# A batched matmul whose output stores are cut into even and odd partitions and spread around the x load

## Chip, cores, metric

One Trainium2 chip, one core. The metric is the device time of one execution in microseconds. A ratio is the mean time of one kernel's fast runs over the mean of the other's of the same rounds, so it is not quite the ratio of the medians that are quoted.

## The reference

```python
b1, b2, m, k, n = 8, 16, 256, 512, 384
# x: (b1, b2, m, k) float32, weight: (b1, b2, k, n) float32
np.matmul(x, weight).astype(np.float32)
```

These are 128 independent products of 256x512 by 512x384. 168 MB are read and 50 MB written.

## The kernel before

Four products (G = 4) make a group, and there are 32 groups. A group has two weight loads of 1.5 MB, one x load of 2 MB and one store of 1.5 MB. All are issued in program order by SyncE on one queue, and the loads run four groups ahead (LAG = 4). VectorE casts the weights, ScalarE casts x, TensorE transposes x through PSUM and multiplies, and ScalarE copies the result to `out_sb`. The matmuls work on 32 columns of the array each, four of them side by side, one for each product of the group; the page has 4096 of them, of 342 ns on average, in 185.1 us of busy TensorE, so they overlap in the records.

```python
def load(e, t, U, s):
    n = t * U + s
    for d in range(G // D):                       # two weight loads
        ...
            e.wait_ge(w_cast, n * (G * S) + ((d + 1) * D * S - 2 * G * S))
        e.dma_start(w_sb[slot][:], ...).then_inc(w_in[slot], 16)
    ...
        e.wait_ge(x_cast, n * T + (1 - XS) * T)   # x of two groups earlier is cast
    e.dma_start(x_sb[s % XS][:], ...).then_inc(x_in[s % XS], 16)

def store(e, t, U, s, pieces=1):
    n = t * U + s
    dram = o_rows[...].rearrange("(p r) n -> p r n", r=R)
    for q in range(pieces):
        rows = slice(q * R // pieces, (q + 1) * R // pieces)
        e.wait_ge(o_copied, n * T + ((q + 1) * T // pieces + BIAS))
        e.dma_start(out=dram[:, rows], in_=out_sb[s % OS][:, rows]).then_inc(o_out[s % OS], 16)

def multiply(e, t, U, s):
    ...                                           # 16 transposes, then:
    for q in range(T):                            # T = 4
        ...
        for rr in range(2):
            for ko in range(KO):                  # KO = 4
                for i in range(G):
                    mine = slice(i * C, (i + 1) * C)          # 32 columns
                    ins = e.matmul(po[...][mine, rr, :N], x_t[...][..., mine, ko % 2],
                                   w_bf[(s * G + i) % WBS][:, ko, :],
                                   start=(ko == 0), stop=(ko == KO - 1))

def on_sync(e):
    for n in range(LAG):
        load(e, 0, NG, n)
    with e.Fori(0, rounds) as t:
        for s in range(U):
            load(e, t, U, LAG + s)
            store(e, t, U, s)
    for n in range(rounds * U, NG):               # the last stores
        ...
```

## Time and profile before

| | before |
|---|---|
| time, median of the runs | 518.4 to 518.7 us, by batch |
| bytes, packets on the queue | 218.11 MB, 18864 |
| share of the queue, mean rate | 99.3%, 422 GB/s |
| busiest compute engine | VectorE, 64% |

A packet is what one DMA engine moves in one go, here one partition's row: 12 KB for weights and outputs (12160 packets in the records), 16 KB for x (4096). Two things of the trace stand outside the page. The packet records have a start and a length for each packet, but not its engine. The landing records have 16 counts for each transfer (2096 for 131 transfers); I take each for one engine's, made as its share lands. I call the time from the first of the 16 to the last the lag of the last engine.

### The profile page before, as it was taken

What the parts mean: (1) busy time and instruction counts of PE and PEld (TensorE: products, weight loads), DVE (VectorE), ACT (ScalarE), POOL (GpSimd) and SP (SyncE); (2) the same over time, 40 slices, a digit from 0 to 9 for tenths busy, and PEclk for the clock granted to TensorE, in tenths of its full rate; (3) what the DMA queues carried; (4) which work ended last, traced back from release to release, by engine and by line L of the source; (5) the groups of instructions that cost most, each with busy time, mean ns of one, the idle gap of its engine ahead of it and who ended that gap; (6) DMA issues with size and microseconds to landing.
All of it is one profiled execution on the core that took longest, in us unless ns stands there. A gap on an engine that the chain in (4) does not pass through costs nothing.

```text
span 517.2 us, 11523 instructions
## 1 busy us (share of the span) xinstructions
PE 306.6 (59%) x4608; PEld 200.6 (39%) x4608; DVE 332.8 (64%) x384; ACT 236.7 (46%) x264; POOL 0.7 (0%) x6
## 2 busy tenths in 40 slices
PE   0478776556665457645577554776446765467752
PEld 0345444334443334433344332444324443244431
DVE  3698875667556676556675566855658656676550
ACT  0465564443644436435355354454444544544441
POOL 0000000000000000000000000000000000000000
PEclk9998877878777887878777778877788877778777
DMA  8999999999999999999999999999999999999996
GB/s 340 430 423 424 424 432 426 429 428 430 432 427 427 427 428 432 429 427 430 426 431 431 426 429 430 427 432 427 427 429 429 427 433 425 430 428 430 429 428 251
DMA packets 18869, 218.18 MB, mean 422 GB/s; under 512 B 2096, under 2 KB 2096, under 8 KB 2608
## 3 DMA queue, kind: packets, MB, share of 16 engines
q1 hardware_dynamic: 18864, 218.11, 99.3%
q8 instruction: 3, 0.05, 0.0%
q14 instruction: 2, 0.02, 0.0%
HBM read 167.77 MB, written 50.33 MB: 422 GB/s over the span
## 4 chain that ended last, share of the span: by engine, by line
DMA 81%; ACT 10%; PE 4%; issue 3%; ACTq 0%; SPq 0%
DMA x_sb<-in_x_dram 81%; ACT x_bf L132 9%; PE po L180 2%; PE pt L166 1%; ACTq L130 0%; ACT out_sb L194 0%; SPq L111 0%; SPq L103 0%; ACT L132 0%; ACTq L193 0%; SPq L282 0%; SPq L55 0%
## 5 line engine op out<-in xcount | busy, mean ns | idle before, releaser
L147 DVE CAST w_bf<-w_sb 64x1536 bf16<-64x1536 f32 x256 | 244.4, 955 | 47.2 <-DMA w_sb<-in_weight_dram 38.5
L166 PE MATMUL pt<-identity,x_bf 128*128 128x128 f32 x512 | 123.7, 425 | 199.3 <-ACT x_bf L132 199.1
L180 PE MATMUL po<-w_bf,x_t 128*32 128x384 bf16 x4096 | 185.1, 342 | 1.0 <-issue 1.0
L166 PEld LDWEIGHTS pt<-identity,x_bf 128*128 128x128 f32 x512 | 91.8, 216 | 232.1 <-issue 218.3
L194 ACT COPY out_sb<-po 128x768 f32<-128x768 f32 x128 | 102.2, 798 | 147.2 <-PE po L180 147.2
L153 DVE COPY x_t<-pt 128x1024 bf16<-128x1024 bf16 x128 | 88.4, 691 | 122.3 <-PE pt L166 121.8
L132 ACT CAST x_bf<-x_sb 128x1024 bf16<-128x1024 f32 x128 | 124.4, 1042 | 80.9 <-DMA x_sb<-in_x_dram 80.8
L180 PEld LDWEIGHTS po<-w_bf,x_t 128*32 128x32 bf16 x4096 | 108.8, 101 | 73.8 <-issue 14.2
L132 ACT ACT_TABLE_LOAD x8 | 10.3, 1283 | 42.9 <-DMA x_sb<-in_x_dram 42.9
masks.py:199 POOL TENSOR_SCALAR_AFFINE_SELECT identity<-identity 128x128 f32<-128x128 f32 x1 | 0.3, 292 | 0.2 <-POOL identity L200 0.2
L200 POOL MEMSET identity<- 128x128 f32 x1 | 0.2, 204 | 0.5 <-SPq L55 0.5
L271 POOL MEMSET const-bfloat16-1.0<- 128x1 bf16 x1 | 0.1, 101 | 0.0
L271 POOL MEMSET const-uint8-127<- 128x1 uint8 x1 | 0.1, 101 | 0.0
L271 POOL MEMSET const-float32-0.0<- 128x1 f32 x1 | 0.1, 98 | 0.2 <-issue 0.2
L271 POOL MEMSET const-float32-1.0<- 128x1 f32 x1 | 0.1, 98 | 0.0
## 6 DMA issues: line engine op xcount, KB each, us to landing
w_sb<-in_weight_dram SPq DMA_DIRECT2D x64, 1536.0 KB, 27.5
x_sb<-in_x_dram SPq DMA_DIRECT2D x32, 2048.0 KB, 27.5
out_dram<-out_sb SPq DMA_DIRECT2D x31, 1536.0 KB, 30.7
out_dram<-out_sb SPq DMA_DIRECT2D x4, 384.0 KB, 5.9
```

What stands on the lines that cost most here:

```text
L132: e.copy(out=x_bf[s % BS][:, rows], in_=x_sb[s % XS][:, rows].rearrange("p r (q s c) -> p r s q c", s=S, c=KO),).then_inc(x_cast, 1)
L147: e.tensor_copy(out=w_bf[(s * G + d * D + a) % WBS][h * HP : (h + 1) * HP], in_=w_sb[slot][a * HP : (a + 1) * HP, h * KO : (h + 1) * KO, : ...
L153: e.tensor_copy(out=x_t[s % TS][:, 2 * q : 2 * q + 2], in_=pt[(s * T + q) % PT][:].bitcast(bf16),).then_inc(t_copied, 1)
L166: ins = e.transpose(pt[(s * T + q) % PT][:, rr, h, :], words[:, 2 * q + rr, h :: KO // 2], identity[:],)
L180: ins = e.matmul(po[(s * T + q) % PO][mine, rr, :N], x_t[s % TS][:, 2 * q + rr, ko // 2, mine, ko % 2], w_bf[(s * G + i) % WBS][:, ko, :], ...
L194: e.copy(out=out_sb[s % OS][:, 2 * q : 2 * q + 2, :], in_=po[(s * T + q) % PO][:, :, :N],).then_inc(o_copied, 1)
L200: e.memset(identity[:], 0.0).then_inc(id_done, 1)
L271: nc = _bacc.Bacc("TRN2", target_bir_lowering=False, num_devices=1)
```

## The change

The writes are spread: half of each store, the even partitions, goes between the weights and x of a later group, the other half, the odd ones, behind x. Below they are the even half and the odd half.

```diff
-    def load(e, t, U, s):
+    def load_w(e, t, U, s):
...
+    def load_x(e, t, U, s):
...
-    def store(e, t, U, s, pieces=1):
+    def store(e, t, U, s, half=None, pieces=1):
...
+        parts = slice(0, P) if half is None else slice(half, P, 2)
...
+            e.dma_start(
+                out=dram[parts, rows], in_=out_sb[s % OS][parts, rows]
+            ).then_inc(o_out[s % OS], 16)
...
             for s in range(U):
-                load(e, t, U, LAG + s)
-                store(e, t, U, s)
+                load_w(e, t, U, LAG + s)
+                store(e, t, U, s, half=0)
+                load_x(e, t, U, LAG + s)
+                store(e, t, U, s, half=1)
```

The counts of `o_out` go from 16 to 32 a store. The stores of the tail are halved too, but the last one still goes in four pieces by rows.

More of the change, by code (lines that the diff above doesn't have):

```diff
@@ L108, in load @@
             ).then_inc(w_in[slot], 16)
+    def load_x(e, t, U, s):
+        n = t * U + s
         if not isinstance(n, int) or n >= XS:
@@ L121, in store @@
             e.wait_ge(o_copied, n * T + ((q + 1) * T // pieces + BIAS))
-            e.dma_start(out=dram[:, rows], in_=out_sb[s % OS][:, rows]).then_inc(
-                o_out[s % OS], 16
-            )
+            e.dma_start(
+                out=dram[parts, rows], in_=out_sb[s % OS][parts, rows]
+            ).then_inc(o_out[s % OS], 16)
     def cast_x(e, t, U, s, q):
@@ L191, in copy_out @@
         if q == 0:
-            e.wait_ge(o_out[s % OS], (t * (U // OS) + s // OS) * 16 + 16)
+            e.wait_ge(o_out[s % OS], (t * (U // OS) + s // OS) * 32 + 32)
         e.wait_ge(p_made, n * T + (q + 1 + BIAS))
@@ L207, in on_sync @@
         for n in range(LAG):
-            load(e, 0, NG, n)
+            load_w(e, 0, NG, n)
+            load_x(e, 0, NG, n)
         rounds = (NG - LAG) // U
@@ L211, in on_sync @@
             for s in range(U):
-                load(e, t, U, LAG + s)
-                store(e, t, U, s)
-        for n in range(rounds * U, NG):
-            if n + LAG < NG:
-                load(e, 0, NG, n + LAG)
-            store(e, 0, NG, n, T if n == NG - 1 else 1)
+                load_w(e, t, U, LAG + s)
+                store(e, t, U, s, half=0)
+                load_x(e, t, U, LAG + s)
+                store(e, t, U, s, half=1)
+        for n in range(rounds * U, NG - 1):
+            for half in range(2):
+                store(e, 0, NG, n, half=half)
+        store(e, 0, NG, NG - 1, pieces=T)
         for s in range(OS):
-            e.wait_ge(o_out[s], 16 + 16 * (NG // OS + (T - 1 if s == (NG - 1) % OS else 0)))
+            e.wait_ge(o_out[s], 32 + 32 * (NG // OS) + (16 * (T - 2) if s == (NG - 1) % OS else 0))
     def on_vector(e):
@@ L242, in on_scalar @@
         for s in range(OS):
-            e.sem_inc(o_out[s], 16)
+            e.sem_inc(o_out[s], 32)
         with e.Fori(0, NG // U) as t:
```

## The prediction

> **What bounds the kernel now.** I read the share of the DMA queue first, then the slices, then the chain of waits, then the issues.
>
> ```profile
> span 517.2 us, 11523 instructions
> ...
> DMA  8999999999999999999999999999999999999996
> GB/s 340 430 423 424 424 432 426 429 428 430 432 427 427 427 428 432 429 427 430 426 431 431 426 429 430 427 432 427 427 429 429 427 433 425 430 428 430 429 428 251
> ...
> q1 hardware_dynamic: 18864, 218.11, 99.3%
> ...
> DMA 81%; ACT 10%; PE 4%; issue 3%; ACTq 0%; SPq 0%
> ```
>
> One queue moves 218.11 MB, and the time of its packets is 99.3% of all 16 DMA engines' span. Every slice but the first and the last holds 423 to 433 GB/s. No compute engine comes near: the busiest, VectorE, has 64%. So this is a DMA-bound kernel, with about 1% outside the packets. The chain "DMA 81%, ACT 10%" must not be read as a latency to be cut: it is a chain of x loads that mostly stand in a queue that is already full, as these two views show.
>
> ```profile
> w_sb<-in_weight_dram SPq DMA_DIRECT2D x64, 1536.0 KB, 27.5
> x_sb<-in_x_dram SPq DMA_DIRECT2D x32, 2048.0 KB, 27.5
> out_dram<-out_sb SPq DMA_DIRECT2D x31, 1536.0 KB, 30.7
> ```
>
> and two rounds of the chain in order of time (start, length):
>
> ```profile
> 433.75 2.94 ACT x_bf L132 x3
> ...
> 436.86 27.73 DMA x_sb<-in_x_dram
> ...
> 465.65 2.94 ACT x_bf L132 x3
> ...
> 468.88 27.67 DMA x_sb<-in_x_dram
> ```
>
> An x load takes 27.7 us from issue to landing, but 2 MB over 16 engines is 8 packets of 16 KB on each, and one such packet takes 0.611 us in the packet records: 4.9 us of work, 22.8 us of queue. The step of that chain, 468.88 - 436.86 = 32.0 us, is the time of two groups (there are two x buffers). Two groups of DMA work are 2 x (16 + 8) packets of 12 KB at 0.460 us and 2 x 8 of 16 KB at 0.611: 22.1 + 9.8 = 31.9 us. The chain runs at the pace of the queue, to 0.1 us.
>
> **The floor.** From the packet records: each engine carries 760 packets of 12 KB (64 weight loads and 31 stores, 8 each), mean 462.3 ns, smallest 459; 256 of 16 KB, mean 614.4, smallest 608; 32 of 3 KB at 121; 131 semaphore packets at 9. Sum: 351.4 + 157.3 + 3.9 + 1.2 = 513.7 us. With every packet at its usual least (460 and 611) it would be 349.6 + 156.4 + 5.1 = 511.1. The first packet starts 2.0 us into the span and the slowest engine's last one ends at about 515.4; 1.8 us of completion follow. In two engines whose packets I could follow one by one, a store packet takes 460.0 ns (461 for the first of eight on one of them) between load packets of 460 to 466: changing direction costs nothing that could be saved. So no reordering of the same bytes can gain more than some 5 us, 1%; 2% would need 508.2.
>
> [...]
>
> **The change part by part.** Removed: 31 stores of 1.5 MB. Added: 62 of 0.75 MB, each four packets of 12 KB on each engine; bytes and packet sizes stay. Each group has one more semaphore packet: 31 x 9 ns = 0.28 us per engine, straight on the bound: 31 x 16 = 496 more packets in the count. SyncE issues 31 more transfers at 0.36 us (the median of a store issue in the trace), 11 us in 517 on a sequencer that mostly waits, with over 20 us of queue below it: 0.
> Moved: the x load of group n+4 now stands behind the wait for group n's outputs and behind half a store. The wait is free: ScalarE copies out group n before it casts x of n+1, and the x load waits anyway for the cast of n+2. In the trace SyncE waits for outputs six times only:
>
> ```profile
> SPq L103 <- DVE w_bf L147: 269.5, 60, 8.6
> SPq L111 <- ACT x_bf L132: 122.5, 30, 5.6
> SPq L122 <- ACT out_sb L194: 35.5, 6, 16.2
> ```
>
> All six and the same 35.5 us appear again when I ask from 440 us on: they are the stores of the tail, after the last load. Half a store ahead of x delays its landing by 4 x 0.46 = 1.84 us once; between two x loads there is the same work as before, so the pace does not change. In the tail the last x lands at 498.4 instead of 496.6, and its chain (11.2 us to the end of the last output copy at 507.7) ends at 509.6. Behind that x the queue still has 3.5 stores and four pieces, 12.9 + 3.9 = 16.8 us, against 11.2 + 1.0 for the chain and the last piece: 4.6 us of room, so the tail stays bound by the queue. Output buffers: a store is issued some 64 us (four groups) before its buffer is written again, and lands 31 us after issue; half a store later changes nothing.
> Sum: 518.5 + 0.3 = 518.8 us.
>
> **Rivals.** (1) [...] The landing records say how far engines are apart: for the x load that lands at about 446 us, 11 of 16 semaphore counts come within 0.93 us, 9 within 0.63, the other five 1.2 to 3.2 us late. [...] I give this 38%, the greatest doubt here.
> (2) A finer mix of reads and writes gains. It could take the excess of packets over their least (513.7 - 511.1 = 2.6 us) and some of the 3 us by which the slowest engine trails. For it: the excess sits in the second weight load and x, not in stores. Worth at most 5 us: 514. Not over 2%.
> (3) x becomes late, and the casts start the chain: x waits for half a store per group and the load slips. Against: 22.8 us of queue ahead of each x load. It would need the queue to run empty; then the slices would fall under 420 GB/s. Some 520 to 525 if at all.
>
> **Range and chances.** Two lumps: 60% around 518.8 (516 to 521), 39% from 530 to 630 with most near 590, and 1% for a gain that the floor excludes. A range of 8 in 10 has to reach into the second lump: 515.5 to 582. Faster by over 2% 0.01, within 2% 0.60, slower 0.39.
>
> **What would show it.** Right: some 19,370 packets, 12 KB packets still 460 ns, middle slices 423 to 433 GB/s, the queue at 99%, SyncE's long waits still on the weight and x casts, x landings still near 28 us. [...] Rival 3: gaps between packets with their durations unchanged. The prediction is wrong if [...]packets fall below 460 ns.

Rival 1 was that engines get in each other's way when a half of 64 partitions is stored, and the 38%, the lump from 530 to 630 us and the upper end of the range, 582, rested on it alone, as the author's guess. That a half gives each engine four packets was assumed too; the records of the changed kernel fit it, with as many packets of 12 KB as before (12160) and 16 landing counts for each half (2592 for 162 transfers).

## The result, and the profile after

The changed kernel takes 524.57 us (524.14 to 524.87, 4 runs), before 518.43; the ratio is 1.0121 (95% interval 1.0106 to 1.0136). That is 6.1 us slower, in the class "within 2%".

The page of the changed kernel, the same lines as shown of the kernel before:

```profile
span 522.9 us, 11610 instructions
...
DMA  8999999999999999999999999999999999999983
GB/s 347 424 428 421 418 427 428 429 430 429 425 435 426 428 430 431 430 424 430 430 430 428 427 428 430 429 430 434 426 426 430 430 430 431 430 427 427 430 362 133
...
q1 hardware_dynamic: 19360, 218.11, 98.3%
```

The middle is unchanged. What changed is the end: the last two slices fall to 362 and 133 GB/s, from 428 and 251 (the page of the kernel before stands in the prediction). Work was left over that not all 16 engines shared. In the packet records the sum over all packets, divided by 16, is 514.0 us, against 513.7 before. So the mean engine has no more to do; some engine must have.

The landing records say which part. This is x, in ns after the first of the 16 engines (decoded from the trace, rows for five of the 32 groups):

```
changed kernel, first engine at us: offsets of the other 15, sorted
 66.192: 60 70 97 107 117 249 529 657 780 829  942  962 2791 2946 2956
 97.923: 58 78 88 103 113 553 617 769 817 931  941 1560 2783 2939 2949
145.550: 40 85 93 101 110 542 616 761 810 931  940 2540 2802 2947 2956
209.040: 20 60 68  78  95 550 623 760 817 940  948 2813 2965 2975 3744
494.583: 46 55 83 100 140 595 657 796 860 965  983 2843 2989 3016 9530
kernel before
 64.340: 18 134 155 175 237 305 422 475 514 692 702  945 2017 2060 2128
493.163: 93 223 270 351 382 548 588 608 879 927 1183 2318 2345 2559 3388
```

Fifteen engines keep their places to some 0.1 us over 400 us. One, which begins at about 0.95 us, falls back by 0.32 us a group, passes the three behind it near 180 us, and is 9.5 us late at the last x. The kernel before has it too, but slower: from about 0.95 to 3.4 us. The growths differ by 8.58 - 2.44 = 6.14 us, and so do the times.

Every x cast waits for the last engine (it lands the last x at 494.583 + 9.530 = 504.11 us, and the cast starts at 504.22), so the chain shows it. In the changed kernel (start, length):

```profile
443.62 28.13 DMA x_sb<-in_x_dram
...
475.93 28.19 DMA x_sb<-in_x_dram
504.22 1.05 ACT x_bf L137
```

The step is 32.3 us in place of 32.0, and the last cast starts at 504.2, not at 496.7. This view puts the time down to "DMA x", although x moves as fast as ever (its 16 KB packets take 611.7 ns on average, 614.4 before); it is the late engine's queue.

What does that engine do slowly? From about 125 us until the tail, the 12 KB packets over 500 ns come in back-to-back runs of four (the first or last of the four sometimes 479 to 499), once a group, and I could follow the late engine's packets back from the last one for 156 packets without a break: its even half takes 516, 521, 535 and 535 ns on average, its odd half 462 to 471. The sum of the first four over 460 is 267 ns, which with some 20 ns of the odd half gives 0.29 us a group, close to the 0.32 that it loses. Two such runs, from the packet records:

```
start us: 480.466 480.981 481.499 482.035 | 496.666 497.175 497.693 498.220
length ns:    519     521     540     531 |     513     521     531     535
```

And what TensorE, ScalarE and VectorE do at the time, in the timeline of the changed kernel:

```profile
476.93 5.81 PE L185 MATMUL po<-w_bf,x_t 128*32 128x384 bf16 x128
...
488.08 3.88 ACT L137 CAST x_bf<-x_sb 128x1024 bf16<-128x1024 f32 x4 [4.49 <-DMA x_sb<-in_x_dram]
...
489.26 3.96 PE L171 MATMUL pt<-identity,x_bf 128*128 128x128 f32 x16 [6.52 <-ACT x_bf L137]
...
493.15 6.22 PE L185 MATMUL po<-w_bf,x_t 128*32 128x384 bf16 x128
```

Both runs lie inside the stage of 128 small matmuls. So do nearly all others: from 110 us on, 104 of the 108 packets of 12 KB that take over 480 ns overlap such a stage, where only 26% of all 12 KB packets do. The odd half, just behind x, is over before that stage starts, and so is the whole store in the kernel before. This stage there, in the same view:

```profile
480.68 3.89 ACT L132 CAST x_bf<-x_sb 128x1024 bf16<-128x1024 f32 x4 [4.36 <-DMA x_sb<-in_x_dram]
...
481.85 3.96 PE L166 MATMUL pt<-identity,x_bf 128*128 128x128 f32 x16 [6.39 <-ACT x_bf L132]
...
485.75 6.23 PE L180 MATMUL po<-w_bf,x_t 128*32 128x384 bf16 x128
```

Here x lands at 480.6, so the store behind it ends on the late engine near 484.3 (8 packets of 460 ns), 1.4 us before the matmuls. Weight packets that run inside the stage are not slowed: in the changed kernel no 12 KB packet between 493.2 and 496.6 us, on any engine, takes over 466 ns.

Only in the tail does the kernel before have the same thing. Its store packets on one engine take 512 to 545 ns from 501.7 to 506.9 us, while the matmuls of the last group run from 501.56 to 506.90. The other engines move their last stores at the same time, and none of their packets takes over 500 ns. In the changed kernel's tail the late engine has nothing but stores, and they pass through all stages of the last group: its 12 KB packets take 460 to 474 ns from 503.6 us on, 472 to 489 from 505.5 to 509.3, 506 to 556 from there to 514.5, then 460 to 474 again. The chain of the last group, before and after (`pt` are the transposes, `po` the matmuls):

```profile
497.83 3.72 PE pt L166 x16
501.56 5.34 PE po L180 x128
...
505.39 3.65 PE pt L171 x16
509.04 5.34 PE po L185 x128
```

So the 16 transposes slow such packets too, only less. This the kernel before has in every group: its store behind x runs into the transposes, and in three groups that I looked at the slow packets there (472 to 484 ns) add up to 0.05 to 0.07 us. That may be most of the 0.09 us a group by which its late engine falls back.

Theory M, then: while the matmul stage runs, one DMA engine moves its store packets 14% slower (about 525 in place of 460 ns); the change put half of each store there; that engine falls back for good, because all engines are full (the queue's share is 98.3%). Its rivals are S, the cut by partition costs something, and L, a store among loads costs something whatever TensorE does.

### The profile page after: what moved, and what is told of

The parts are those of the page before. It is cut to its first block, busy times and chain, and to the rows that moved or that the text cites. A ratio compares the mean times of both kernels' runs of the same rounds, so it can differ in the third digit from the quotient of the medians.

```text
span 522.9 us, 11610 instructions
## 1 busy us (share of the span) xinstructions
PE 310.3 (59%) x4608; PEld 200.5 (38%) x4608; DVE 332.8 (64%) x384; ACT 237.3 (45%) x264; POOL 0.7 (0%) x6
## 3 DMA queue, kind: packets, MB, share of 16 engines
q1 hardware_dynamic: 19360, 218.11, 98.3%
## 4 chain that ended last, share of the span: by engine, by line
DMA 82%; ACT 9%; PE 4%; issue 3%; SPq 0%; ACTq 0%
DMA x_sb<-in_x_dram 82%; ACT x_bf L137 9%; PE po L185 2%; PE pt L171 1%; ACTq L135 0%; ACT out_sb L199 0%; SPq L115 0%; SPq L104 0%; ACT L137 0%; ACTq L198 0%; SPq L290 0%; SPq L56 0%
## 5 line engine op out<-in xcount | busy, mean ns | idle before, releaser
L185 PE MATMUL po<-w_bf,x_t 128*32 128x384 bf16 x4096 | 189.0, 347 | 0.0
```

Of the source, the lines that this page charges most:

```text
L185: ins = e.matmul(po[(s * T + q) % PO][mine, rr, :N], x_t[s % TS][:, 2 * q + rr, ko // 2, mine, ko % 2], w_bf[(s * G + i) % WBS][:, ko, :], ...
```

## The experiments

All are timed against the kernel before, whose medians in the batches were 518.57, 518.67 and 518.67 us. The edits start from the changed kernel unless said otherwise. "Lag" is that of the last engine at the last x; it was 3.39 us before and 9.53 in the changed kernel.

**Whole store between weights and x.** No cut; the semaphore counts are those of the kernel before.

```diff
                 load_w(e, t, U, LAG + s)
-                store(e, t, U, s, half=0)
+                store(e, t, U, s)
                 load_x(e, t, U, LAG + s)
-                store(e, t, U, s, half=1)
```

> The whole store (128 partitions, one transfer) stands between the weights and x of the later group; nothing is split. Theory M (one late DMA engine moves its store packets in about 525 ns in place of 460 while the matmuls of L180 run, and the place in the queue puts a store there): all 8 store packets of a group are hit in place of 4, so about 28 x 8 x 65 ns = 14.6 us over the kernel before, some 531 to 533. Rival S (the cut into even and odd partitions costs): no cut, so 518.5. Rival L (a store among loads costs something, whatever the matmuls do): also slower, 525 to 533, not told from M by this run.

Measured 530.38 us, ratio 1.0226, just under the 531 to 533 of M. The lag is 15.24 us: 11.85 more than before, and the time is 11.81 more. The lag grows 0.52 us a group, eight packets of 65 ns. So the cut is not needed for the loss. Its page has the same middle and a worse end (the kernel before ends with 428 and 251 here):

```profile
GB/s 343 428 425 425 424 431 421 427 431 430 430 426 428 426 428 429 435 424 430 428 427 428 434 424 430 428 429 428 434 424 430 429 426 429 433 422 430 430 188 132
```

**Both halves behind x.** The cut stays, the place is the old one.

```diff
                 load_w(e, t, U, LAG + s)
-                store(e, t, U, s, half=0)
                 load_x(e, t, U, LAG + s)
+                store(e, t, U, s, half=0)
                 store(e, t, U, s, half=1)
```

> The store is cut into even and odd partitions, but both halves stand behind x, where the store stood before. Theory M: no store packet meets the matmuls, so 518.8 (the kernel before and 0.3 for 496 semaphore packets). Rival S (the cut costs): 524.5 as in the changed kernel. Rival L: 518.8 as M.

Measured 519.47 us, ratio 1.0017; lag 3.66. S falls: the cut into even and odd partitions costs some 0.9 us (0 to 1.7 by the interval of the ratio), of which 0.3 would be the added semaphore packets as predicted and 0.3 is the lag.

**One wide matmul for four narrow ones** (wrong result).

```diff
-                    for i in range(G):
-                        mine = slice(i * C, (i + 1) * C)
-                        ins = e.matmul(
-                            po[(s * T + q) % PO][mine, rr, :N],
-                            x_t[s % TS][:, 2 * q + rr, ko // 2, mine, ko % 2],
-                            w_bf[(s * G + i) % WBS][:, ko, :],
+                    ins = e.matmul(
+                        po[(s * T + q) % PO][:, rr, :N],
+                        x_t[s % TS][:, 2 * q + rr, ko // 2, :, ko % 2],
+                        w_bf[(s * G + ko) % WBS][:, ko, :],
```

> The changed kernel with a wrong result on purpose: one matmul of 128 columns in place of four of 32 columns that run side by side, so a quarter of the PE instructions, with the matmul stage about as long as before (some 5.3 us). Theory M in the form 'the number of PE instructions does it': the excess falls to about a quarter, 65 to 16 ns a packet, 520 to 521. M in the form 'TensorE streaming its data does it': 524.5 still. Rival L: 524.5 still.

Measured 519.31 us, ratio 1.0012; lag 4.32. That is below even the 520 to 521 of M. L falls: the half store stands among loads as in the changed kernel, and the loss is nearly gone. The stage takes about as long as before (6.62 and 6.19 us below, 5.81 and 6.22 in the views of the changed kernel above), with a quarter of the instructions. It also streams a quarter of the columns, which the expectation overlooked: of four narrow matmuls side by side, each streams 384 of its own.

```profile
138.56 6.62 PE L183 MATMUL po<-w_bf,x_t 128*128 128x384 bf16 x32
...
153.09 6.19 PE L183 MATMUL po<-w_bf,x_t 128*128 128x384 bf16 x32
```

The slow packets that remain take 473 to 498 ns, and 481 on average in the ten groups where all four of the late engine's stand out. So the number of instructions matters, or the data that they stream, or that four narrow matmuls run side by side; this run does not tell these apart. Side by side is not needed, though: the slow packets here, and those beside the transposes above, have none of it.

**A quarter of the matmuls** (wrong result).

```diff
-                for ko in range(KO):
+                for ko in range(1):
...
-                            stop=(ko == KO - 1),
+                            stop=True,
```

> The changed kernel with a wrong result on purpose: only the first of the four ko steps, so the matmul stage takes about 1.4 us in place of 5.8 and is over before the late engine reaches its even half. Theory M, both forms: no excess, 518.8 or a little less (a shorter last chain). Rival L (a store among loads costs, whatever the matmuls do): 524.

Measured 518.48 us, ratio 0.9997; lag 3.38. As M has it: with the stage out of the way, the order and the cut of the change cost nothing. L falls a second time.

**As many instructions with little data** (wrong result).

```diff
+                        cols = slice(0, N) if ko == 0 else slice(N, N + 8)
                         ins = e.matmul(
-                            po[(s * T + q) % PO][mine, rr, :N],
+                            po[(s * T + q) % PO][mine, rr, cols],
...
-                            w_bf[(s * G + i) % WBS][:, ko, :],
-                            start=(ko == 0),
-                            stop=(ko == KO - 1),
+                            w_bf[(s * G + i) % WBS][:, ko, : cols.stop - cols.start],
+                            start=True,
+                            stop=True,
```

> The changed kernel with a wrong result on purpose: as many matmuls and weight loads as in the changed kernel (128 and 128 a group), but three of four stream 8 columns in place of 384, so TensorE moves about a quarter of the data in the stage. The wide kernel had a quarter of the instructions and half the excess of a packet or less. Theory I (the rate of PE instructions slows the late engine's stores): store packets that meet the stage take 520 ns or more, and with at least 4 us of stage the time comes back to 521 to 525. Theory D (the data that TensorE streams does it): like the run with a quarter of the matmuls, 518.5, packets up to 500 at most.

Measured 520.30 us, ratio 1.0032; lag 4.87. The expectation of the time (521 to 525, on condition of 4 us of stage) was missed, as the stage is shorter and has gaps. In the timeline the 128 matmuls take 1.12 + 1.34 us here:

```profile
202.10 1.12 PE L186 MATMUL po<-w_bf,x_t 128*32 128x384 bf16 x64
...
203.78 1.34 PE L186 MATMUL po<-w_bf,x_t 128*32 128x384 bf16 x64 [0.56 <-ACT out_sb L200]
```

(The line names the first of two shapes.) The late engine's store now only touches the stage, so few packets are hit, but these harder than in the changed kernel: 564 ns at 204.64 us, 606 at 140.56, 611 at 269.06, and in the last group 695 at 505.72. The matmul stage of the changed kernel has 128 matmuls and 128 weight loads in 5.34 us where it runs without stalls (the last group), so 48 instructions per us, and its packets take about 525 ns. Here it is 128 in 1.34 us, 96 per us. Theory D, the data that TensorE streams, falls: about a quarter of the data, in the burst about half as many columns per us (16 matmuls of 384 and 48 of 8 in 1.34 us, against 128 of 384 in 5.34), and packets up to 695. The rate of PE instructions (theory I of the expectation) fits: in proportion to 65 ns at 48 per us, 96 would give 590 ns, and the 12 of the wide kernel 476, where it had 481. It is no exact law: the transposes, 9 per us with their weight loads, should give 472, and in the tail they had 472 to 489.

**Halves by rows at the places of the change.** All 128 partitions, packets of 6 KB.

```diff
-        parts = slice(0, P) if half is None else slice(half, P, 2)
...
+            if half is not None:
+                rows = slice(half * R // 2, (half + 1) * R // 2)
...
-                out=dram[parts, rows], in_=out_sb[s % OS][parts, rows]
+                out=dram[:, rows], in_=out_sb[s % OS][:, rows]
```

> The halves are cut by rows and not by partitions (all 128 partitions, packets of 6 KB, four rows each), at the places of the changed kernel. Theory M (the place counts, not the cut): 524.5, 8 packets of 6 KB a group slowed by the same share. Rival S [...]: 518.8.

Measured 524.96 us, ratio 1.0119; lag 9.49. Within 0.2 us of the changed kernel, as differences from the kernel before (6.3 and 6.1): another cut, the same places, the same loss. The slow 6 KB packets mostly take 258 to 291 ns, the median is 234.

**Contiguous halves behind x.** The order of the run with both halves behind x, and:

```diff
-        parts = slice(0, P) if half is None else slice(half, P, 2)
+        parts = slice(0, P) if half is None else slice(half * P // 2, (half + 1) * P // 2)
```

> Both halves behind x, as in the run where both stood there and the time was 519.5, but cut into partitions 0 to 63 and 64 to 127. [...]1.84 us more a half, 62 halves, +114 us at worst: 600 to 632. [...]519.5.

Measured 525.22 us (521.23 to 526.21), ratio 1.0111 (1.0062 to 1.0159). The expectation has two cases: 600 to 632 if each half takes up to twice its 4 x 460 ns, and 519.5 if it is not slowed. The first was badly missed, and 519.5 too. The cut does cost, though: 57 store and weight packets of 874 between 40 and 80 us take over 520 ns, some up to 2.2 us, but between 300 and 495 us not one of 4674. Meanwhile the engines have moved apart: at an x landing at 64.4 us, 13 of 16 come within 0.71 us and the last at 2.36; at 256.7 us they are spread over 5.46 us, and at 478.9 over 5.66. My guess is that some engines hinder one another until they are apart, and then no more, so that the loss does not come back with each of the 62 halves. That they do, and by what, was not shown. The last stores are slow again: 28 of 509 packets after 495 us are over 520 ns.

**Whole store between the two weight loads.** A dose between the old place and the early one (against the run with the whole store early):

```diff
-                load_w(e, t, U, LAG + s)
+                load_w(e, t, U, LAG + s, [0])
                 store(e, t, U, s)
+                load_w(e, t, U, LAG + s, [1])
                 load_x(e, t, U, LAG + s)
```

> The whole store between the two weight loads of the later group, so on the late engine it starts 3.7 us after x lands and ends at 7.4, while the matmul stage runs from about 5.1 to 10.9 us after x lands. Theory M: some 5 of 8 store packets meet the stage, 28 x 5 x 65 ns = 9.1 us, 527.6. Rival L (a store among loads costs whatever meets it): as the whole store between weights and x, 530.4.

Measured 522.42 us, ratio 1.0070; lag 7.32, 3.93 more than before, and 3.75 us more time. The direction is right and L falls again, as this is a whole store among loads at 3.8 us and not at 11.8; the size is not. The late engine's growth, (7.32 - 0.59) / 27 = 0.25 us a group (it is 0.59 us behind at 68.1 us), is about four packets of 65 ns over the run, not five more than before. My estimate of the overlap took one fixed distance from x to the matmuls for all groups; the trace has a single packet over 500 ns from 110 to 230 us, and later, before the tail, up to five a group.

**Two attempts to beat both.** The store whole, inside a split x load, so that it should fall behind the matmuls:

```diff
+    CUT = 6                                    # 4 in the second attempt
-    def load_x(e, t, U, s):
+    def load_x(e, t, U, s, part):
...
+        rows = slice(0, CUT) if part == 0 else slice(CUT, R)
...
-                store(e, t, U, s, half=0)
-                load_x(e, t, U, LAG + s)
-                store(e, t, U, s, half=1)
+                load_x(e, t, U, LAG + s, 0)
+                store(e, t, U, s)
+                load_x(e, t, U, LAG + s, 1)
```

> A version that might beat both. The store is whole; x of the later group goes as two transfers by rows, six and two of eight, and the store stands between them. Counted from the landing of x on the late engine, the two weight loads take 0 to 7.4 us, six rows of x to 11.0, the store 11.0 to 14.7, two rows of x to 15.9: the store meets neither the matmuls (5.1 to 10.9) nor the transposes (1.2 to 5.1 after the next landing). Theory M: the late engine no longer falls behind. In the kernel before it does so by about 0.1 us a group, to 3.4 us at the last x; so up to 2.5 us of gain, 516 to 518. If the place of the store has nothing to do with it: 519 or more (512 more packets).

> As the run before, but x is cut four and four: the store takes 9.8 to 13.5 us after the landing and so meets the last 1.1 us of the matmuls, some two packets of eight. Theory M: 28 x 2 x 65 ns = 3.6 us worse than the version with six and two, 519.5 to 521.5. If the place has nothing to do with it: the same time as that one.

Measured 524.09 us (ratio 1.0108) and 526.16 (1.0144). Neither beats anything. First, cutting x makes the packets dearer: a 4 KB packet takes 159 ns, so a row of 12 and one of 4 KB take 619 at the medians in place of the 613 of one 16 KB packet, and the sum per engine rises from 513.7 to 517.2 us with 6 + 2, and to 516.9 with 4 + 4. Second, the store still meets the matmuls, as they run later than I had put them: from 110 to 495 us, 62 of the 12 KB packets with 6 + 2 still take over 480 ns, and 94 with 4 + 4. That the version which overlaps more is 2.1 us slower is as M has it, against 3.6 expected. The kernel before remains the fastest.

Time and lag beside one another, as differences from the kernel before, in us, for the runs whose packets are the same size, without the contiguous halves:

```
                              time    lag at the last x
changed kernel                +6.1    +6.1
whole store early            +11.8   +11.9
both halves behind x          +0.9    +0.3
wide matmuls                  +0.7    +0.9
a quarter of the matmuls      -0.1     0.0
many instructions, few data   +1.6    +1.5
whole store in the middle     +3.8    +3.9
```

## Why the prediction was right, and where it was not

- **Range and class: right.** 524.57 lies in 515.5 to 582.0, and the change is within 2%. But the point, 518.8, was 5.8 us short. The range was wide for the sake of rival 1, and 524.57 lies in neither of the two lumps that it was made of (516 to 521, 530 to 630): that the range held it was luck.
- **Floor: right.** Nothing was gained in time. The mean packet sum went from 513.7 to 514.0 us. The 0.3 us are those predicted for the semaphore packets, as two other changes cancel: the 12 KB packets went from a mean of 462.3 to 463.2 ns, 0.7 us more per engine, and the 16 KB ones from 614.4 to 611.7, 0.7 us less. The latter is the kind of gain that rival 2 (a finer mix) had in mind, at about a quarter of its 2.6 us. There are 19360 packets on the queue, 496 more, as predicted. The cut alone at the old place cost some 0.9 us.
- **Waits of SyncE: right.** The wait for outputs is again in six waits, 32.9 us in place of 35.5, and the weight and x casts keep the long ones. A half store takes 0.49 us to issue and not 0.36, which cost nothing either. In this view of who waited for whom in the changed kernel:

```profile
SPq L104 <- DVE w_bf L152: 241.6, 60, 8.6
SPq L115 <- ACT x_bf L137: 134.7, 30, 6.5
SPq L127 <- ACT out_sb L199: 32.9, 6, 15.5
```

- **Failed step: "12 KB packets still 460 ns".** It holds for the median packet (460 in both kernels), but the kernel ends with its slowest engine, and on that one the even half takes 516 to 535. In the sum, a term for four packets of a group on one engine, 4 x 65 ns x 28 groups = 7.3 us, was missing; the late engine in fact fell back by 6.1 us more than before. The trace of the kernel before had the sign of it: I saw that the slowest engine trailed by 3 us and took it for a fixed offset, where it grew from about 0.95 to 3.4 us; and I did not look at the slow store packets of its tail against the timeline.
- **Failed in consequence: the tail.** The last x landed at 504.1, not 498.4 us: the lag is 6.1 us larger than I had it, and the first engine 0.4 us earlier. The "4.6 us of room" were used up for the 15 engines, which ran dry (the slices of 362 and 133 GB/s), while the late engine's own queue ended at 521.1.
- **Rival 1 (engines in each other's way): not what happened.** The even and odd halves together cost 0.9 us when both stood behind x (519.47 us), and the late engine, as far as it was followed, moved four packets of each half, of 460 ns or little more outside the matmuls and transposes. That a loss would come back at each half is doubtful besides: with the contiguous halves, which did cost 6.6 us, no packet of 12 KB took over 520 ns from 300 to 495 us.
- **Rival 3 (x late): right in look, wrong in cause.** x did become late, but the queue never ran empty, and it is the late engine and not the place of x in the queue.

**What stays open.** Why PE instructions slow one DMA engine's stores (from 460 to about 525 ns a packet beside the changed kernel's matmuls). Fetching them by DMA is not it, as far as the trace records this: its instruction queues (q8 and q14) have six packets in the changed kernel's span, 0.07 MB, the last at 79.7 us. Nor is it shown why the weight loads beside the same matmuls are not slowed (at most 466 ns from 493.2 to 496.6 us). Every run here, timed ones too, comes with a recorded span and granted clock, so there is no run without recording to compare with. Which of the 16 engines it is was not found either.

## What to carry to other kernels

Here all DMA engines were full, and the kernel ended with the slowest one, so look at the spread of landings over the run and not only at the queue's mean share: 98 to 99% of the mean hid an engine that lost 0.3 us a group. The place of a transfer in the full queue also fixed which compute stage it ran beside; here a store belongs directly behind x (518.4 us, against 524.6 with half of it before x and 530.4 with all of it), where it is over before the burst of small matmuls. Cutting the store bought nothing; with the order kept it cost some 0.9 us by even and odd partitions, and 6.6 us by contiguous halves.
